# A block of seven products in a gated MLP: two weight quadrants loaded earlier, two down pieces moved ahead of the last product, the gate turned in one

## The chip, the cores and the metric

The kernel runs on one core of a Trainium2 chip. The metric is the device time of one execution in microseconds (us), taken as the median of several runs. One execution was also profiled by the hardware; its span runs from the first to the last instruction, and its own time is a little longer than its span. Engines are named as in the profile: PE does matmuls (PEld loads their weights), DVE and ACT work on tensors element by element, POOL does little here, SP issues nearly all DMAs.

## The reference

The reference is an encoder of two layers on 256 tokens of 1024 channels, in float32. Each layer has a token mixer and then a gated MLP; only the MLP matters here:

```python
def _conv_ffn(xn, w_up, conv_w, conv_b, w_down):
    a, gval = jnp.split(xn @ w_up, 2, axis=-1)
    a = lax.conv_general_dilated(a, conv_w[:, None, :], window_strides=(1,),
                                 padding=((CONV_WIDTH // 2, CONV_WIDTH // 2),),
                                 dimension_numbers=('NWC', 'WIO', 'NWC'),
                                 feature_group_count=D_FF) + conv_b
    return (jax.nn.gelu(a) * gval) @ w_down
```

`w_up` is 1024 x 5632 (2816 columns for `a`, 2816 for the gate), `w_down` 2816 x 1024. `setup_inputs` draws all weights at random.

## The kernel before

**Two parts for every number.** A float32 weight is read from memory as a `raw` tile (1 MB: two pieces of 128 x 1024), and each piece is split into a rounded part `wh` (a cast on ACT, line 252) and the rest `wl` (a subtraction on DVE, line 254). PE multiplies with both: wh by x's high part, wl by x's high part, wh by x's low part. So one piece costs ACT a cast, DVE a subtraction and PE 12 matmuls of 512 columns (6 where only one half of the tokens is multiplied). There are 3 raw buffers and 5 buffers each for `wh` and `wl`; a piece can be split only when PE has finished with the piece five places earlier. A raw load with a tag goes into another, named tile and takes none of the 3 buffers.

**Order.** The middle of each layer is written out by hand: `tc.manual_schedule()` keeps every engine's instructions in the order in which the Python code makes them. The order of the weight pieces is the order of the `W.use` calls, and the order of the loads that of the `W.add` calls (through `rows`); a load is issued as soon as it is within reach of the piece that is split next. SP issues DMAs in that order and stands still at one whose buffer is not free.

**The MLP's groups.** `MLP_GROUPS` lists them: `g` and `a` groups are 512 columns of the gate half and of the `a` half of `w_up` (four pieces, line 750), `w` is the block, `b` a mixed rest group, `d` are pieces of `w_down`. After a group its result is turned on DVE (line 804, "crossing"), written to DRAM in chunks (line 809) and read back with channels on partitions (line 816, into `zga` and `zg`). For each pair of 128-channel chunks f there are then five steps at places that `PAIR_PLACES` gives: on ACT `fetch_up` (lines 1487 and 1489) and the GELU (1497), on DVE `neighbours` (1493, 1494), `gate` (1501), then a cast on ACT (1509) and a rest on DVE (1510). A "place" is one piece of work of PE; the first is 8.

**The block.** Group 3 of both halves together is a 2 x 2 product of quadrants, computed with seven products instead of eight (`block` for the weights, `block_units` for the products, line 1579): "11", "T1", "22", "T2", "21", "T3", "T4". T1 to T4 take sums of weight quadrants, which DVE makes in the raw tiles (line 342) just before the piece is split. Quadrants "11" and "12" (first row block of `w_up`; 11 of the gate half, 12 of the `a` half) lie in the tagged tiles `ybig` and `at2`; T1 needs both. Four PSUM banks of the pool `mmp` serve groups and block; the block's are p (11, 21: first half of the gate), t and q. `add(0)`, `add(1)` on DVE (line 1604, tile `kept`) add a bank to a kept one and turn the result; T3 and T4 write on into the bank q that `add(0)` and `add(1)` read. `BLOCK` gives the order of the products and of eight `w_down` pieces "d" (lines 667 to 669, `res_ps`) in between, and the dictionary `after` what follows each product.

Of the kernel before, what the change touches and what calls it, by code (L numbers as in the profile page):

```python
# [26 lines left out]
DFF = 2816  # L27
# [262 lines left out]
def encoder(ctx, tc, x, w_in, w_pool, pool_scale, w_a, w_b, w_o, norm1, norm2, w_up, conv_w,  # L290
# [11 lines left out]
    W = Weights(tc, wpool, big, sm)  # L302
# [16 lines left out]

    def block(w, down, n):  # L320

        def quadrant(k, c0, tag=None):
            return rows(w, k * 512, 4, c0, 512, tag)

        gate, act = DFF + n * 512, n * 512
        made = {"11": quadrant(0, gate, "ybig"), "12": quadrant(0, act, "at2")}
        d = rows(down, 0) + rows(down, 2 * P)
        made["22"] = quadrant(1, act)
        d += rows(down, 4 * P)
        made["21"] = quadrant(1, gate)  # L330
        d += rows(down, 6 * P)
# [3 lines left out]
        def raw(name, j):  # L335
            return W.raw[made[name][0][0]][:, 2 * j : 2 * j + 2]
# [11 lines left out]
        k = 0  # L348
        for unit in BLOCK:
            if unit == "d":  # L350
                W.use([d[k]])
                k += 1
                continue
            name, j = unit
            if name in SUMS:
                sum_later(len(W.pieces), SUMS[name], j)
            if name in terms:
                W.use([(d[k][0], lambda t, name=name, j=j: raw(name, j), (2, 512))])
            else:
                W.use([made[name][j]])  # L360

    first_up = []
    for l in range(DEPTH):
# [659 lines left out]
    for l in range(DEPTH):  # L1023
# [527 lines left out]
        def block_units(n):  # L1551
# [50 lines left out]
            def add(t):  # L1602
# [75 lines left out]
```

## Time and profile before

| what | value |
|---|---|
| median of 3 runs | 862.76 us (861.73 to 863.35) |
| the profiled execution | 863.14 us, its span 861.3 us |
| granted TensorE clock, mean | 0.997 |
| DVE `wl` (L254) | 286 of 1217 ns, 343.8 us busy |
| ACT `wh` (L252) | 286 of 1048 ns, 296.0 us busy |
| chain that ended last | PE 80%, DVE 10%, DMA 5% |
| DMA | 214.03 MB, mean 248 GB/s |

Busy times overlap between engines, so they don't add up to the span. In a timeline row the first number is the start in us from the start of the span, the second the time from the first instruction's start to the last one's end, then engine, line, operation and tiles, and in brackets the idle time before it with what ended it. In a row of windows, after the stretch and its length, stand the busy time and count of PE, PEld, DVE, ACT and POOL, then PE's granted clock, the DMA engines' busy share and the GB/s moved. A row of the chain has start, length and what.

### The profile page before, as it was taken

How to read it: one execution, taken by the hardware profiler on the slowest of the kernel's cores; microseconds unless marked ns; L12 is line 12 of the kernel's file. 1: busy time of each engine (PE TensorE's matmuls, PEld its weight loads, DVE VectorE, ACT ScalarE, POOL GpSimd, SP SyncE). 2: the span in 40 equal slices, each digit the busy share in tenths (PEclk: the TensorE clock that was granted, in tenths of full speed). 3: DMA queues.
4: the chain of work that ended last, by engine and by line, in shares of the span. 5: the costliest groups of instructions: out<-in, count | busy, mean ns of one | idle time of the engine just before them, and what ended most of it. 6: DMA issues, size and time to landing. Idle time of an engine off the chain costs nothing.

```text
span 861.3 us, 10959 instructions
## 1 busy us (share of the span) xinstructions
PE 845.2 (98%) x3901; PEld 702.3 (82%) x3901; DVE 645.2 (75%) x838; ACT 522.6 (61%) x757; POOL 35.1 (4%) x96
## 2 busy tenths in 40 slices
PE   9999999999999989999999999999999999899997
PEld 7888888888888868788888888888888888687886
DVE  6958877766777679887765687868567876998774
ACT  7735556644565766677645454577454656767683
POOL 1710000000010000000010000000000100000000
PEclk9999999999999999999999999999999999999999
DMA  8699986886738866788736899768776499667861
GB/s 302 218 299 304 325 269 210 280 281 225 251 137 305 289 239 218 231 292 284 260 127 199 265 276 328 250 223 269 242 264 248 147 308 313 215 215 246 295 241 50
DMA packets 147967, 214.03 MB, mean 248 GB/s; under 512 B 7800, under 2 KB 69184, under 8 KB 147912
## 3 DMA queue, kind: packets, MB, share of 16 engines
q1 hardware_dynamic: 147480, 212.67, 74.6%
q8 instruction: 31, 0.51, 0.2%
q10 hardware_dynamic: 432, 0.66, 0.2%
q14 instruction: 24, 0.20, 0.1%
HBM read 186.02 MB, written 27.28 MB: 248 GB/s over the span
## 4 chain that ended last, share of the span: by engine, by line
PE 80%; DVE 10%; DMA 5%; ACT 2%; issue 2%; SPq 0%; POOL 0%; ACTq 0%; DVEq 0%; POOLq 0%
PE t_ps L750 50%; PE v_ps L750 6%; DVE wl L254 5%; PE res_ps L668 5%; PE res_ps L667 5%; PE res_ps L669 5%; DMA raw<-in_w_up_dram 3%; PE v_ps L1003 3%; DVE raw L342 2%; PE pool_ps L654 1%; PE v_ps L902 1%; DMA crossing<-crossing 1%; PE t_ps L1579 1%; PE o_ps L1286 1%; PE s_ps L1238 1%
## 5 line engine op out<-in xcount | busy, mean ns | idle before, releaser
L254 DVE TENSOR_TENSOR wl<-raw,wh 128x1024 fp32r<-128x1024 f32 x286 | 343.8, 1217 | 109.5 <-ACT wh L252 108.6
L750 PE MATMUL t_ps<-wh,x 128*128 128x512 f32 x1280 | 399.5, 390 | 0.0
L252 ACT CAST wh<-raw 128x1024 fp32r<-128x1024 f32 x286 | 296.0, 1048 | 169.5 <-PE t_ps L750 103.0
L750 PEld LDWEIGHTS t_ps<-wh,x 128*128 128x128 f32 x1280 | 240.3, 188 | 49.8
L750 PE MATMUL t_ps<-wl,x 128*128 128x512 f32 x640 | 249.1, 389 | 0.0
L750 PEld LDWEIGHTS t_ps<-wl,x 128*128 128x128 f32 x640 | 120.2, 188 | 25.1 <-DVE wl L254 0.2
L668 PE MATMUL res_ps<-wl,actq 128*128 128x512 f32 (+1 forms) x184 | 70.1, 381 | 1.7 <-DVE wl L254 1.7
L667 PE MATMUL res_ps<-wh,actq 128*128 128x512 f32 (+1 forms) x184 | 70.2, 382 | 1.3 <-ACT wh L252 1.3
L669 PE MATMUL res_ps<-wh,actk 128*128 128x512 f32 (+1 forms) x184 | 69.3, 380 | 0.0
L668 PEld LDWEIGHTS res_ps<-wl,actq 128*128 128x128 f32 x184 | 34.6, 188 | 8.9 <-DVE wl L254 2.3
L667 PEld LDWEIGHTS res_ps<-wh,actq 128*128 128x128 f32 x184 | 34.6, 188 | 8.8 <-ACT wh L252 2.2
L750 PE MATMUL t_ps<-wh,po 128*128 128x512 f32 x128 | 41.4, 395 | 0.0
L669 PEld LDWEIGHTS res_ps<-wh,actk 128*128 128x128 f32 x184 | 34.6, 188 | 6.5
L1489 ACT ACTIVATE a<-zga,prm 128x256 f32<-128x256 f32 x80 | 38.9, 512 | 0.0
L544 POOL TENSOR_SCALAR ss<-ss 128x1 f32<-128x1 f32 x8 | 2.1, 265 | 779.4 <-ACT junk L537 779.4
L804 DVE STREAM_TRANSPOSE crossing<-t_ps 128x512 f32<-128x512 f32 x36 | 23.9, 694 | 6.7 <-DMA crossing<-crossing 6.7
L342 DVE TENSOR_TENSOR raw<-raw,raw 128x1024 f32<-128x1024 f32 x16 | 19.5, 1217 | 12.7 <-DMA raw<-in_w_up_dram 12.7
L750 PEld LDWEIGHTS t_ps<-wh,po 128*128 128x128 f32 x128 | 24.0, 188 | 4.9
L1497 ACT ACTIVATE y<-y 128x512 f32<-128x512 f32 x22 | 13.9, 633 | 21.3 <-DVE y L1494 21.3
L667 PE MATMUL res_ps<-wh,m 128*128 128x512 f32 (+1 forms) x72 | 26.5, 367 | 0.0
L668 PE MATMUL res_ps<-wl,m 128*128 128x512 f32 (+1 forms) x72 | 26.3, 365 | 0.0
L669 PE MATMUL res_ps<-wh,m 128*128 128x512 f32 (+1 forms) x72 | 26.0, 366 | 0.0
(211 smaller groups left out, 1067.4 us busy)
## 6 DMA issues: line engine op xcount, KB each, us to landing
raw<-in_w_in_dram SPq DMA_DIRECT2D x58, 1024.0 KB
raw<-in_w_up_dram SPq DMA_DIRECT2D x40, 1024.0 KB
raw<-in_w_down_dram SPq DMA_DIRECT2D x22, 1024.0 KB
crossing<-crossing SPq DMA_DIRECT2D x22, 512.0 KB
crossing<-way SPq DMA_DIRECT2D x16, 512.0 KB
raw<-in_w_a_dram SPq DMA_DIRECT2D x8, 1024.0 KB
raw<-in_w_o_dram SPq DMA_DIRECT2D x8, 1024.0 KB
zga<-crossing SPq DMA_DIRECT2D x40, 128.0 KB
```

The source lines that it names most:

```text
L252: inst = nc.scalar.copy(out=h, in_=src)
L254: inst = self.rests[i] = nc.vector.tensor_sub(out=l, in0=src, in1=h.bitcast(F32))
L342: nc.vector.tensor_sub(out=raw(name, j), in0=raw(one, j), in1=raw(other, j))
L654: nc.tensor.matmul(out, w(k), x, start=(steps is first and k == 0), stop=(steps is last and k == nk - 1), skip_group_check=turns["rest"],)
L667: nc.tensor.matmul(ps, ah, wh, start=first, stop=False, skip_group_check=on)
L668: nc.tensor.matmul(ps, ah, wl, start=False, stop=False, skip_group_check=on)
L669: nc.tensor.matmul(ps, al, wh, start=False, stop=last, skip_group_check=on)
L750: nc.tensor.matmul(ps, x2[:, 2 * n + j, part, t, :], w[:, j, :], start=(n + m == 0), stop=(n == last and m == 5),)
L804: nc.vector.transpose(out=y.rearrange("p q c j -> p c q j"), in_=rows)
L1003: nc.tensor.matmul(ps[t], a[:, k, t, :], w[:, j, :], start=(k + m == 0), stop=(k == KD - 1 and m == 2),)
L1489: nc.scalar.mul(out=out, in_=a, mul=row(j, c))
L1497: nc.scalar.activation(t["y"], t["y"], AF.Gelu_apprx_tanh)
```

## The change

Four edits, the same in both layers.

1. The loads of quadrants 11 and 12 are added before the pieces of group `a` 2 instead of behind group `g` 2; `quadrant` and `first_quadrants` are taken out of `block` for that.
2. In `BLOCK` the last "d" moves from behind T4 to ahead of it: T3, d, d, T4 instead of T3, d, T4, d.
3. The first half of the gate (bank p) is no longer turned behind T3 but behind T4, together with the second half.
4. In `PAIR_PLACES` the pair f = 8 moves from places (39, 41), inside the block, to (46, 48), behind it; f = 10, 12 and 14 move by one slot each, f = 14 now having (55, 57).

```diff
 PAIR_PLACES = (
-    (11, 14), (14, 16), (19, 22), (21, 23), (39, 41), (46, 48), (49, 51), (52, 54), (60, 62), (63, 65), (58, 60),
+    (11, 14), (14, 16), (19, 22), (21, 23), (46, 48), (49, 51), (52, 54), (55, 57), (60, 62), (63, 65), (58, 60),
 )
 BLOCK = (
     ("11", 0), ("11", 1), "d", ("T1", 0), ("T1", 1), "d", "d", ("22", 0), ("22", 1), "d", ("T2", 0), ("T2", 1), "d",
-    ("21", 0), ("21", 1), "d", ("T3", 0), ("T3", 1), "d", ("T4", 0), ("T4", 1), "d",
+    ("21", 0), ("21", 1), "d", ("T3", 0), ("T3", 1), "d", "d", ("T4", 0), ("T4", 1),
 )
...
-    def block(w, down, n):
-
-        def quadrant(k, c0, tag=None):
-            return rows(w, k * 512, 4, c0, 512, tag)
-
-        gate, act = DFF + n * 512, n * 512
-        made = {"11": quadrant(0, gate, "ybig"), "12": quadrant(0, act, "at2")}
+    def quadrant(w, n, k, gate, tag=None):
+        return rows(w, k * 512, 4, gate * DFF + n * 512, 512, tag)
+
+    def first_quadrants(w, n):
+        return {"11": quadrant(w, n, 0, 1, "ybig"), "12": quadrant(w, n, 0, 0, "at2")}
+
+    def block(w, down, n, made):
+        made = dict(made)
...
         for kind, n in MLP_GROUPS:
+            if (kind, n) == ("a", 2):
+                corner = first_quadrants(w_up[l], 3)
             if kind == "w":
-                block(w_up[l], w_down[l], n)
+                block(w_up[l], w_down[l], n, corner)
...
-                "T3": (lambda: add(1), lambda: turn("g", 0, banks["p"])), "T4": (lambda: turn("g", 1, banks["q"]),),
+                "T3": (lambda: add(1),), "T4": (lambda: turn("g", 0, banks["p"]), lambda: turn("g", 1, banks["q"])),
```

On SP, at the start of the first layer's MLP, before (2444 to 2535 are raw tiles of `w_up` for the groups a 1, g 1 and the first of a 2; `crossing` is a group's result on its way out, `zga` its way back):

```order
L412 DMA gain<-in_norm_dram 128x1024
L171 DMA raw_2444<-in_w_up_dram 128x4x512
L809 DMA crossing<-crossing 128x2x512
L816 DMA zga<-crossing 32x8x128 x4
L171 DMA raw_2466<-in_w_up_dram 128x4x512
L171 DMA raw_2500<-in_w_up_dram 128x4x512
L809 DMA crossing<-crossing 128x2x512
L171 DMA raw_2535<-in_w_up_dram 128x4x512
```

and with the change, in the same place on SP, where 2535 and 2537 are now quadrants 11 and 12 and 2539 is the first tile of a 2:

```order
L415 DMA gain<-in_norm_dram 128x1024
L171 DMA raw_2535<-in_w_up_dram 128x4x512
L171 DMA raw_2444<-in_w_up_dram 128x4x512
L812 DMA crossing<-crossing 128x2x512
L171 DMA raw_2537<-in_w_up_dram 128x4x512
L819 DMA zga<-crossing 32x8x128 x4
L171 DMA raw_2466<-in_w_up_dram 128x4x512
L171 DMA raw_2500<-in_w_up_dram 128x4x512
L812 DMA crossing<-crossing 128x2x512
L171 DMA raw_2539<-in_w_up_dram 128x4x512
```

Quadrant 11 now stands ahead of the last raw tile of a 1, and quadrant 12 ahead of the reads that bring group a 0 back.

On SP, shortly ahead of the block, before (2662 is the last tile of g 2, 2719 and 2725 are quadrants 11 and 12, 2727 and 2764 hold the first four down pieces):

```order
L171 DMA raw_2662<-in_w_up_dram 128x4x512
L809 DMA crossing<-crossing 128x2x512
L171 DMA raw_2719<-in_w_up_dram 128x4x512
L816 DMA zg<-crossing 32x8x128 x4
L171 DMA raw_2725<-in_w_up_dram 128x4x512
L171 DMA raw_2727<-in_w_down_dram 128x2x1024
L171 DMA raw_2764<-in_w_down_dram 128x2x1024
L809 DMA crossing<-crossing 128x2x512
```

and with the change, in the same place on SP (2666 is the last tile of g 2, 2723 and 2764 hold the down pieces):

```order
L171 DMA raw_2666<-in_w_up_dram 128x4x512
L812 DMA crossing<-crossing 128x2x512
L171 DMA raw_2723<-in_w_down_dram 128x2x1024
L819 DMA zg<-crossing 32x8x128 x4
L171 DMA raw_2764<-in_w_down_dram 128x2x1024
L812 DMA crossing<-crossing 128x2x512
```

Both quadrant loads are gone from here, and a down tile has the place of the first.

On DVE, at the end of the first layer's block, before (3126 and 3151 are T4's two pieces, 3164 the last d's; `y`, `g` and `actk` are the pair f = 8; the last `kept` is `add(1)`; the transposes behind it turn its result and bank p):

```order
L254 TENSOR_TENSOR wl_3126<-raw_2725,wh_3125 128x1024
L1493 TENSOR_TENSOR y<-y,a_3141 128x2x255
L1494 TENSOR_TENSOR y<-y,a_3143 128x2x255
L254 TENSOR_TENSOR wl_3151<-raw_2725,wh_3150 128x1024
L1501 TENSOR_TENSOR g<-y,zg 128x512
L254 TENSOR_TENSOR wl_3164<-raw_3006,wh_3163 128x1024
L1510 TENSOR_TENSOR actk_2427<-g,actq_2425 128x512
L1604 TENSOR_TENSOR kept<-t_ps,kept 128x512
L804 STREAM_TRANSPOSE crossing<-kept 128x4x4x32
L804 STREAM_TRANSPOSE crossing<-t_ps 128x4x4x32
```

and with the change, in the same place on DVE (3126 is the last d's piece, 3142 and 3152 are T4's, 3162 to 3216 the four of the group b):

```order
L254 TENSOR_TENSOR wl_3126<-raw_3006,wh_3125 128x1024
L254 TENSOR_TENSOR wl_3142<-raw_2537,wh_3141 128x1024
L254 TENSOR_TENSOR wl_3152<-raw_2537,wh_3151 128x1024
L1607 TENSOR_TENSOR kept<-t_ps,kept 128x512
L807 STREAM_TRANSPOSE crossing<-kept 128x4x4x32
L254 TENSOR_TENSOR wl_3162<-raw_3087,wh_3161 128x1024
L254 TENSOR_TENSOR wl_3188<-raw_3087,wh_3187 128x1024
L254 TENSOR_TENSOR wl_3204<-raw_3090,wh_3203 128x1024
L254 TENSOR_TENSOR wl_3216<-raw_3090,wh_3215 128x1024
L807 STREAM_TRANSPOSE crossing<-t_ps 128x4x4x32 x2
```

The four instructions of f = 8 have left the stretch ahead of `add(1)`, and the gate's two transposes stand together behind the pieces of group b.

More of the change, by code (lines that the diff above doesn't have):

```diff
@@ L318, in of_both @@
         )
[L320 to L326 removed]
+    def quadrant(w, n, k, gate, tag=None):
[4 more added lines that the diff above has]
+        made = dict(made)
         d = rows(down, 0) + rows(down, 2 * P)
[L328 removed]
+        made["22"] = quadrant(w, n, 1, 0)
         d += rows(down, 4 * P)
[L330 removed]
+        made["21"] = quadrant(w, n, 1, 1)
         d += rows(down, 6 * P)
@@ L356, in block @@
                 sum_later(len(W.pieces), SUMS[name], j)
-            if name in terms:
-                W.use([(d[k][0], lambda t, name=name, j=j: raw(name, j), (2, 512))])
+            if name in ("22", "21"):
+                W.use([made[name][j]])
             else:
-                W.use([made[name][j]])
+                W.use([(d[min(k, 7)][0], lambda t, name=name, j=j: raw(name, j), (2, 512))])
     first_up = []
```

## The prediction

> **What bounds the kernel now.** I read the totals first, then the chain that ended last, then PE's own timeline.
>
> ```profile
> span 861.3 us, 10959 instructions
> PE 845.2 (98%) x3901; PEld 702.3 (82%) x3901; DVE 645.2 (75%) x838; ACT 522.6 (61%) x757; POOL 35.1 (4%) x96
> ...
> 257.87 40.42 PE t_ps L750 x179
> 361.00 32.64 PE t_ps L750 x144
> ```
>
> The first two lines are totals, the other two pieces of the chain. PE is the bound, so only a change that takes idle or slow time from PE can shorten the kernel. The last row gives PE's pitch when nothing is in its way: 32.64 us / 144 = 0.2267 us from one matmul to the next. With that pitch each stage's PE time is known, and what a stage takes beyond it is lost. In the block PE does 14 half products of 6 matmuls and 8 down pieces of 12, so 180 matmuls, or 40.8 us. The first and last of them, in both layers, and the rows at which PE waited:
>
> ```profile
> 312.11 0.39 PE L1579 MATMUL t_ps<-wh,x 128*128 128x512 f32 x1
> 316.40 0.50 PE L667 MATMUL res_ps<-wh,actq 128*128 128x512 f32 x1 [0.87 <-ACT wh L252]
> 317.73 0.50 PE L668 MATMUL res_ps<-wl,actq 128*128 128x512 f32 x1 [0.82 <-DVE wl L254]
> 321.38 0.47 PE L1579 MATMUL t_ps<-wh,sx 128*128 128x512 f32 x1 [0.86 <-DVE crossing L804]
> 351.25 0.39 PE L669 MATMUL res_ps<-wh,actk 128*128 128x512 f32 x1
> 353.72 0.77 PE L1579 MATMUL t_ps<-wh,x 128*128 128x512 f32 x1 [2.08 <-DVE kept L1604]
> 360.83 0.39 PE L750 MATMUL t_ps<-wh,x 128*128 128x512 f32 x1
> ...
> 737.83 0.39 PE L1579 MATMUL t_ps<-wh,x 128*128 128x512 f32 x1
> 746.16 0.47 PE L1579 MATMUL t_ps<-wh,sx 128*128 128x512 f32 x1 [0.87 <-DVE crossing L804]
> 778.49 0.47 PE L1579 MATMUL t_ps<-wh,x 128*128 128x512 f32 x1 [2.08 <-DVE kept L1604]
> 784.05 0.39 PE L750 MATMUL t_ps<-wh,x 128*128 128x512 f32 x1
> ```
>
> The block takes 360.83 - 312.11 = 48.72 us in the first layer and 784.05 - 737.83 = 46.22 us in the second, so **7.9 and 5.4 us are lost, 13.3 us together**. Three places hold them. *Start*: up to T1's first matmul (321.38 and 746.16) there are 24 matmuls, 5.44 us; PE took 9.27 and 8.33, a loss of 3.8 and 2.9. *End*: from there to T4's first matmul (353.72 and 778.49) there are 132 matmuls, 29.92 us; it took 32.34 and 32.33, a loss of 2.4 in each. *After T4's start*, 24 matmuls: 7.11 and 5.56 for 5.44, a loss of 1.7 in the first layer and 0.1 in the second. The windows name that last one, by the clock column (the third number from the end; the first row is the whole block of the first layer):
>
> ```profile
> 312.10:360.80 48.70, 44.01 (x181) 34.52 (x180) 44.11 (x48) 34.01 (x45) 0.00 (x0) 0.96 0.62 202
> 353.55:356.95 3.40, 3.23 (x8) 2.59 (x9) 0.73 (x2) 0.52 (x2) 0.00 (x0) 0.52 0.52 163
> 778.40:781.80 3.40, 3.31 (x15) 2.75 (x16) 0.69 (x1) 1.42 (x3) 0.00 (x0) 1.00 0.54 167
> ```
>
> After the same wait the granted clock was about half for 3.4 us in the first layer, and full in the second.
>
> The Trainium skill, "TensorE: Matmul & The Clock Gate", Part 1 (The HAM clock gate), says that the clock is halved after an idle window of about 3.4 us that runs freely, so that the same kernel can meet it or not. Here a wait of 2.46 us between matmul starts (351.25 to 353.72) was enough once and not the other time. By that rule a wait that stays may cost 1.7 us in either layer, where the rows have it in one.
>
> Why PE waited is told by DVE, where both waits end:
>
> ```profile
> 305.10 1.23 DVE L342 TENSOR_TENSOR raw<-raw,raw 128x1024 f32<-128x1024 f32 x1 [6.80 <-DMA raw<-in_w_up_dram]
> 320.53 1.30 DVE L804 STREAM_TRANSPOSE crossing<-t_ps 128x512 f32<-128x512 f32 x2
> 348.02 0.68 DVE L1493 TENSOR_TENSOR y<-y,a 128x510 f32<-128x510 f32 x1
> 352.29 0.68 DVE L1510 TENSOR_TENSOR actk<-g,actq 128x512 fp32r<-128x512 f32 x1
> 352.89 0.68 DVE L1604 TENSOR_TENSOR kept<-t_ps,kept 128x512 f32<-128x512 f32 x1
> 729.88 1.22 DVE L342 TENSOR_TENSOR raw<-raw,raw 128x1024 f32<-128x1024 f32 x1 [5.86 <-DMA raw<-in_w_up_dram]
> 745.30 1.30 DVE L804 STREAM_TRANSPOSE crossing<-t_ps 128x512 f32<-128x512 f32 x2
> ```
>
> T1's first sum stood idle 6.80 us (5.86 in the second layer) for quadrant 12, and held up everything that follows it on DVE, down to the transposes of group g 2 that free T1's bank. At the other end `add(1)` ran at 352.89, behind f = 8, and T4 may not write into its bank before.
>
> **Part 1, the early loads: the start.** Without that DMA wait DVE's chain moves up 6.80 and 5.86 us. The first of g 2's transposes (half of 1.30, so 0.65) then ends at 320.53 + 0.65 - 6.80 = 314.4, and in the second layer at 745.30 + 0.65 - 5.86 = 740.1. PE at full pitch wants T1's bank at 312.11 + 5.44 = 317.55, and at 737.83 + 5.44 = 743.27. Both are met with 3 us to spare; g 2's own matmuls end where the block begins, so they don't hold the transposes. The cast and rest at which PE waited at 316.40 and 317.73 hang on the same chain. So the start's 3.8 + 2.9 = **6.7 us go**. What is late next is nothing at T1; DVE would have to slip another 3 us.
>
> What the two loads cost where they now stand is told by the chain's row for group a 0, SP's timeline, three windows (the last two numbers are the DMA share and GB/s), ACT's timeline and the page's groups (the number behind the comma is the mean in ns):
>
> ```profile
> 252.40 5.47 PE v_ps L750 x24
> ...
> 257.25 0.37 SPq L171 DMA_DIRECT2D raw<-in_w_up_dram  x1
> 259.61 0.37 SPq L809 DMA_DIRECT2D crossing<-crossing  x1
> 263.74 1.81 SPq L816 DMA_DIRECT2D zga<-crossing  x4
> 265.66 1.23 SPq L171 DMA_DIRECT2D raw<-in_w_up_dram  x2
> ...
> 258.90:263.00 4.10, 4.10 (x20) 3.40 (x19) 4.10 (x7) 3.12 (x4) 0.00 (x0) 1.00 0.96 369
> 263.00:264.90 1.90, 1.90 (x10) 1.59 (x9) 1.90 (x3) 1.05 (x1) 0.00 (x0) 1.00 0.05 16
> 267.00:276.00 9.00, 9.00 (x41) 7.47 (x40) 5.93 (x7) 3.23 (x4) 0.00 (x0) 1.00 1.01 381
> ...
> 270.86 2.00 ACT L252 CAST wh<-raw 128x1024 fp32r<-128x1024 f32 x2 [3.69 <-DMA raw<-in_w_up_dram]
> ...
> L254 DVE TENSOR_TENSOR wl<-raw,wh 128x1024 fp32r<-128x1024 f32 x286 | 343.8, 1217 | 109.5 <-ACT wh L252 108.6
> L252 ACT CAST wh<-raw 128x1024 fp32r<-128x1024 f32 x286 | 296.0, 1048 | 169.5 <-PE t_ps L750 103.0
> ```
>
> Quadrant 11 needs `ybig`, which holds the second of group a 0's four pieces. PE leaves it half way through the 24 matmuls that start at 252.40, at about 255.1, before SP issues the next raw load at 257.25: SP's stop there costs nothing. `at2` holds the third piece and is free about 256.5, before SP has passed the crossing at 259.61. A load is 1.05 MB, at 369 to 381 GB/s 2.8 us. The first finds the queue empty from 255.1; the second falls into the hole at 263.0 to 264.9 (share 0.05), where SP waits for a crossing to land, and pushes the reads behind it by 2.8 - 1.9 = 0.9 us. At worst both stand fully in the way, 5.6 us. The first raw tile of g 1 is then ready for ACT at 270.86 + 5.6 = 276.5 instead of 270.86. PE starts g 1 at 257.87 plus 96 matmuls, 279.6; cast and rest (1048 and 1217 ns) need 2.3 us, so the slack is 279.6 - 2.3 - 270.86 = **6.4 us**. I take 0 for PE; the lower bound is 0, since PE has no idle time there to give back, and the upper one, both loads fully in the way, is 0 too, as 5.6 is under 6.4. The second layer does the same work in the same order, and I take the same. Ahead of the block the queue loses the same two loads.
>
> **Part 2, the second d ahead of T4, and f = 8 out of the block: the end.** Between T3 and T4 PE now has two down pieces, 5.44 us, instead of one, 2.72. The wait there was 2.4 us, so the second d covers it by itself, with 0.3 to spare. f = 8 takes four DVE instructions of 0.68 us, starting at 348.02 and ending with the row at 352.29, from in front of `add(1)`: 2.4 to 2.7 us more. And DVE arrives up to 6.8 us earlier. What bounds `add(1)` then is PE: T4's second piece waits for T3's first buffer, which PE leaves after 138 matmuls, at 312.11 + 31.28 = 343.4; cast, rest and `kept` (1.05 + 1.22 + 0.68) put its end at 346.4. PE wants T4 after 168 matmuls, at 350.2. Margin 3.8 us, so the end's 2.4 + 2.4 go, and with the wait the half clock and the 0.1 behind it: **6.6 us**.
>
> **Part 3, the gate turned in one.** The same two transposes, later. They hold two banks until just behind T4; by the order of instructions group a 4 is the first that waits for them, a whole group b (48 matmuls, 10.9 us) later, and two transposes take 1.30. Cost 0; without that cover 1.3 us a layer.
>
> **Part 4, f = 8 behind the block.** Its work goes into groups b, a 4 and g 4, three windows of 10.9 us (DVE's busy time is the third, ACT's the fourth after the length), with the longest of its ACT instructions from the page's groups:
>
> ```profile
> 360.80:371.70 10.90, 10.90 (x49) 9.01 (x48) 10.16 (x12) 9.33 (x16) 0.00 (x0) 1.00 0.96 308
> 371.70:382.60 10.90, 10.90 (x50) 9.02 (x49) 7.68 (x10) 8.39 (x15) 0.00 (x0) 1.00 0.74 267
> 382.60:393.50 10.90, 10.90 (x50) 9.03 (x49) 8.41 (x10) 5.68 (x7) 0.00 (x0) 1.00 0.81 277
> ...
> L1497 ACT ACTIVATE y<-y 128x512 f32<-128x512 f32 x22 | 13.9, 633 | 21.3 <-DVE y L1494 21.3
> ```
>
> DVE has 26.3 of 32.7 us there and gets 2.7; ACT has 23.4 and gets eight instructions of at most 0.633, so under 5.1. Both still fit (29.0 and 28.5), and PE, which does not wait there, comes in with up to five pieces split ahead. Cost 0; with the cover gone, at most ACT's 5.1 a layer.
>
> **The sum.** 6.7 + 6.6 = 13.3 us, all that PE loses in the two blocks, against the profiled execution's 863.14 us (its span 861.3 and 1.8 around it): **849.8 us**. The median of the runs before, 862.76, is 0.4 us lower; a run without the half clock would be 1.7 lower, so the ratio to the median is a little smaller.
>
> **Rivals.**
> *Half of it.* Only the end goes, because something other than quadrant 12 also holds T1's sum; or only the start, because DVE, 44.11 us busy of 48.70 in the block, can't keep its lead. That gives 863.14 - 6.6 = 856.5 or 863.14 - 6.7 = 856.4. Against the first: the wait at 305.10 is put down to a DMA of `w_up`. Against the second: the second d alone covers the end. 0.08 and 0.07.
> *The edit does not do what it says*: SP or the queue brings the quadrants no sooner in effect and DVE's lag moves to the next sum. 863, for which only DVE's load speaks: 0.05.
> *The early loads starve g 1, and the kernel is slower.* From 257 to 276 the queue is full (share 1.01), so a delay may not be made up. It decides at 6.4 us: beyond, PE waits in both layers, and the whole gain is gone once the delay is 6.4 + 6.65 = 13.1 us, with the two loads at about 160 GB/s instead of 370. At a delay of 14 us the time is 849.8 + 2 x 7.6 = 865.0. The hole at 263 and the 6.4 us speak against it: 0.05.
>
> The Trainium skill, "DMA: Bandwidth & Descriptors", section "Queues, rings and completion order", says that descriptors of one ring are consumed in order, so a load put in front delays all that SP issued behind it. That is this rival's mechanism; no row before separates it from SP's own waits. By the page's limit for one core's memory, about 358 GB/s (Specifications), the two loads would take an estimated 5.9 us instead of 5.6; the row at 381 GB/s is above that limit. Neither reaches the slack.
>
> **Chances and range.** Forecast, both ends go: 0.75, with a range of its own of 848.8 to 852 (0.2% or 1.7 us is about what a measurement of this kernel can tell from no change; small waits of some tenths may stay, and the median before is 0.4 lower). The halves reach to 857.0, which together is 0.90; a cut at 852 would leave out 0.25. So 848.8 to 857.0. Faster by over 0.2%: 0.75 + 0.15 = 0.90; within: 0.05; slower: 0.05.
>
> **What would show it.** Right: T1's sum on DVE has no DMA wait ahead of it; T1's first matmul comes 5.4 to 5.6 us after the block's first; `kept` ends over 3 us ahead of T4; the block's windows show 40.8 to 41.2 us and a full clock. Wrong: PE rows in g 1 or a 2 that wait for a cast (early loads too dear), an idle row on DVE at the sum that another load ended, a wait at T4 for `kept`, or one in a 4 or g 4 for f = 8.

## The result and the profile after

| | median | runs |
|---|---|---|
| before | 863.06 us (861.73 to 867.08) | 4 |
| changed | 849.89 us (849.66 to 851.33) | 4 |

The ratio is 0.9843, with a 95% interval of 0.9809 to 0.9878: 1.6% faster. Forecast was 849.8 us. The profiled execution of the changed kernel took 851.33 us (span 849.5 and 1.8 around it), which makes it the longest of its four. So its trace shows a little that the other runs may not have. Of all runs reported below one was slow, the second of six of "loads and f = 8" (1320.13 us at a granted clock of 0.60), and its ratio leaves it out.

The totals of the changed kernel and the engines of its chain of waits:

```profile
span 849.5 us, 10951 instructions
PE 840.6 (99%) x3901; PEld 700.9 (83%) x3901; DVE 645.6 (76%) x838; ACT 523.8 (62%) x757; POOL 34.0 (4%) x96
...
PE 89%; DMA 4%; DVE 4%; ACT 1%; issue 1%; SPq 0%; POOL 0%; ACTq 0%; DVEq 0%; POOLq 0%
```

PE has 89% of the chain where it had 80%, and DVE 4% where it had 10%. PE's timeline has the same places as before: the block's first matmul, the waits, T1's first, T4's first and the first behind the block (lines of the changed kernel are higher by 3):

```profile
312.03 0.39 PE L1582 MATMUL t_ps<-wh,x 128*128 128x512 f32 x1
315.38 0.50 PE L671 MATMUL res_ps<-wl,actq 128*128 128x512 f32 x1 [0.25 <-DVE wl L254]
319.04 0.47 PE L1582 MATMUL t_ps<-wh,sx 128*128 128x512 f32 x1 [0.87 <-DVE crossing L807]
351.83 0.39 PE L1582 MATMUL t_ps<-wh,x 128*128 128x512 f32 x1
354.55 0.39 PE L753 MATMUL t_ps<-wh,x 128*128 128x512 f32 x1
...
731.51 0.39 PE L1582 MATMUL t_ps<-wh,x 128*128 128x512 f32 x1
736.96 0.39 PE L1582 MATMUL t_ps<-wh,sx 128*128 128x512 f32 x1
769.60 0.39 PE L1582 MATMUL t_ps<-wh,x 128*128 128x512 f32 x1
772.32 0.39 PE L753 MATMUL t_ps<-wh,x 128*128 128x512 f32 x1
```

In the second layer no row waits: the block takes 772.32 - 731.51 = 40.81 us, which is 180 matmuls at full pitch. In the first it takes 42.52. T1 comes 7.01 us after the first matmul instead of 5.44, so 1.57 us of start loss are left, and some 0.14 behind it. T4 waits in neither layer. The windows of the two blocks say the same (clock third from the end):

```profile
312.03:354.55 42.52, 41.40 (x182) 33.55 (x180) 40.33 (x42) 28.34 (x33) 0.00 (x0) 1.00 0.64 207
731.51:772.32 40.81, 40.81 (x182) 33.79 (x181) 37.44 (x38) 25.28 (x27) 0.00 (x0) 1.00 0.60 202
```

No half clock is left in either block. Together they took 94.94 us before and take 83.33 now: 11.61 of the 11.81 us between the two profiled executions (863.14 and 851.33).

DVE's timeline at T1's first sum, at g 2's transposes and at `add(1)`, in both layers:

```profile
302.78 1.22 DVE L343 TENSOR_TENSOR raw<-raw,raw 128x1024 f32<-128x1024 f32 x1
318.19 1.31 DVE L807 STREAM_TRANSPOSE crossing<-t_ps 128x512 f32<-128x512 f32 x2
347.95 0.68 DVE L1607 TENSOR_TENSOR kept<-t_ps,kept 128x512 f32<-128x512 f32 x1
...
718.60 1.22 DVE L343 TENSOR_TENSOR raw<-raw,raw 128x1024 f32<-128x1024 f32 x1
734.01 1.30 DVE L807 STREAM_TRANSPOSE crossing<-t_ps 128x512 f32<-128x512 f32 x2
765.22 0.68 DVE L1607 TENSOR_TENSOR kept<-t_ps,kept 128x512 f32<-128x512 f32 x1
```

T1's sum no longer waits for a DMA. But in the first layer it starts at 302.78, only 2.3 us sooner than the 305.10 of before, where the prediction had 6.8. Why is seen on SP, first before the change and then with it:

```profile
263.74 1.81 SPq L816 DMA_DIRECT2D zga<-crossing  x4
269.96 0.37 SPq L809 DMA_DIRECT2D crossing<-crossing  x1
274.69 1.81 SPq L816 DMA_DIRECT2D zg<-crossing  x4
276.59 0.40 SPq L171 DMA_DIRECT2D raw<-in_w_up_dram  x1
```

```profile
266.08 1.81 SPq L819 DMA_DIRECT2D zga<-crossing  x4
269.88 0.37 SPq L812 DMA_DIRECT2D crossing<-crossing  x1
279.83 1.81 SPq L819 DMA_DIRECT2D zg<-crossing  x4
281.74 0.40 SPq L171 DMA_DIRECT2D raw<-in_w_up_dram  x1
```

SP issues the second `crossing` at the same time as before, but the reads `zg`, which wait until it has landed, go out 5.1 us later, and the tile of a 2 behind them too. ACT's timeline in the changed kernel shows the tiles landing late:

```profile
275.87 2.00 ACT L252 CAST wh<-raw 128x1024 fp32r<-128x1024 f32 x2 [8.78 <-DMA raw<-in_w_up_dram]
290.61 1.05 ACT L252 CAST wh<-raw 128x1024 fp32r<-128x1024 f32 x1 [3.56 <-DMA raw<-in_w_up_dram]
```

The first cast of g 1 is at 275.87 instead of 270.86. The cast of the third piece of a 2, at 290.61, waited for a DMA as well, and T1's sum follows it 12.2 us later. Before the change that cast was 5.5 us sooner and waited for PE:

```profile
285.11 1.05 ACT L252 CAST wh<-raw 128x1024 fp32r<-128x1024 f32 x1 [0.65 <-PE t_ps L750]
```

PE did not wait in g 1 or a 2. So two of the signs that the prediction named for being right, T1 within 5.6 us and a block of at most 41.2 us, are missing in the first layer of this profile and there in the second.

### The profile page after: what moved, and what is told of

It is laid out like the page before. It is cut to its first block, busy times and chain, and to the rows that moved or that the text cites. A ratio compares the mean times of both kernels' runs of the same rounds, so it can differ in the third digit from the quotient of the medians.

```text
span 849.5 us, 10951 instructions
## 1 busy us (share of the span) xinstructions
PE 840.6 (99%) x3901; PEld 700.9 (83%) x3901; DVE 645.6 (76%) x838; ACT 523.8 (62%) x757; POOL 34.0 (4%) x96
## 4 chain that ended last, share of the span: by engine, by line
PE 89%; DMA 4%; DVE 4%; ACT 1%; issue 1%; SPq 0%; POOL 0%; ACTq 0%; DVEq 0%; POOLq 0%
PE t_ps L753 53%; PE res_ps L670 6%; PE res_ps L671 6%; PE res_ps L672 6%; PE v_ps L753 6%; PE t_ps L1582 4%; PE v_ps L1006 3%; DMA raw<-in_w_up_dram 2%; DVE wl L254 1%; PE pool_ps L657 1%; PE v_ps L905 1%; DMA crossing<-crossing 1%; PE o_ps L1289 1%; PE s_ps L1241 1%; PE s_ps L1236 1%; PE o_ps L1285 1%
## 5 line engine op out<-in xcount | busy, mean ns | idle before, releaser
L540 ACT ACTIVATE junk<-h 128x512 f32<-128x512 f32 (+1 forms) x19 | 10.5, 554 | 25.2 <-DVE h L562 25.0
L1496 DVE TENSOR_TENSOR y<-y,a 128x510 f32<-128x510 f32 x22 | 14.9, 679 | 14.1 <-ACT y L1490 14.1
L753 PE MATMUL v_ps<-wh,x 128*128 128x512 f32 x80 | 25.7, 392 | 0.0
```

Of the source, the lines that this page charges most:

```text
L540: nc.scalar.activation(junk[:, 0 : cc.stop - cc.start], h[:, t, cc], AF.Square, scale=D**-0.5, accum_out=ss[:, n : n + 1],)
L753: nc.tensor.matmul(ps, x2[:, 2 * n + j, part, t, :], w[:, j, :], start=(n + m == 0), stop=(n == last and m == 5),)
L1496: nc.vector.tensor_add(out=y[:, :, 1:], in0=y[:, :, 1:], in1=t["a0"][:, :, : S - 1])
```

## The experiments

All times are medians; each ratio is against runs of the kernel before on the same chip, whose medians were 864.7 to 865.2 us there (863.06 for the first profile of the changed kernel). "Start" is the time from the block's first matmul to T1's first, less 5.44 us. "Lead" is how long before the block's first matmul DVE starts T1's first sum. Both stand for the first / second layer of the profiled execution. "End only", "second d only" and "f = 8 only" are the changed kernel with both quadrant loads put back to the block, and with the other edits that are not named taken back; the edits below are shown against the kernel before.

| kernel | median us | ratio (95%) | lead | start loss |
|---|---|---|---|---|
| before, first profile | 863.06 | | 7.01 / 7.95 | 3.84 / 2.88 |
| changed, first profile | 849.89 | 0.9843 (0.9809 to 0.9878) | 9.25 / 12.91 | 1.57 / 0 |
| changed, second | 849.87 | 0.9833 (0.9809 to 0.9857) | 11.44 / 11.84 | 0 / 0 |
| changed, third | 850.34 | 0.9842 (0.9819 to 0.9864) | 11.77 / 10.09 | 0 / 0.76 |
| loads only | 855.97 | 0.9907 (0.9885 to 0.9929) | 11.31 / 8.79 | 0 / 2.03 |
| end only | 858.15 | 0.9930 (0.9910 to 0.9951) | 7.06 / 7.13 | 3.78 / 4.27 |
| second d only | 863.59 | 0.9990 (0.9971 to 1.0008) | 7.91 / 7.56 | 2.94 / 3.29 |
| f = 8 only | 857.82 | 0.9926 (0.9902 to 0.9950) | 6.27 / 7.58 | 5.13 / 3.28 |
| changed, f = 8 in the block | 850.93 | 0.9847 (0.9823 to 0.9871) | 11.68 / 11.20 | 0 / 0 |
| loads and f = 8 | 850.17 | 0.9830 (0.9807 to 0.9854) | 11.05 / 13.74 | 0 / 0 |
| changed, gate turned apart | 850.75 | 0.9844 (0.9822 to 0.9866) | 11.23 / 10.49 | 0 / 0.34 |
| both quadrants at g 2 | 852.70 | 0.9859 (0.9834 to 0.9884) | 9.59 / 9.65 | 1.25 / 1.19 |
| quadrant 11 at a 2, 12 at g 2 | 853.71 | 0.9887 (0.9858 to 0.9916) | 11.33 / 9.66 | 0 / 1.18 |
| early loads doubled | 862.97 | 0.9978 (0.9959 to 0.9996) | 8.57 / 8.05 | 2.26 / 2.78 |

### The early loads alone

```diff
         for kind, n in MLP_GROUPS:
+            if (kind, n) == ("a", 2):
+                corner = first_quadrants(w_up[l], 3)
...
-                block(w_up[l], w_down[l], n)
+                block(w_up[l], w_down[l], n, corner)
```

> The early quadrant loads alone; the order of T3, d, T4, d, the gate's turns and f = 8 stay as before. Theory (start and end are two separate losses): in both layers the wait at T1 goes or shrinks to the 1.3 us that the changed kernel kept in its first layer, while the wait at T4 for `kept` stays at 1.0 to 2.4 us; 863.1 - 6.7 = 856.4, up to 858. Rival 1 (DVE's lead alone would have been enough, the end's edits do nothing): the waits at T4 go too, 850 to 852. Rival 2 (DVE's rate through the block sets its end, so what PE gains at T1 it waits for at T4): the waits at T4 grow to 5 us or more and the time stays at 862 to 863.

855.97 us, 0.9907: the theory's size, and the waits at T4 stayed. The timelines of DVE and PE at T4 in the first layer:

```profile
348.50 0.69 DVE L1607 TENSOR_TENSOR kept<-t_ps,kept 128x512 f32<-128x512 f32 x1
...
349.33 0.47 PE L1582 MATMUL t_ps<-wh,x 128*128 128x512 f32 x1 [1.80 <-DVE kept L1607]
```

PE's waits in this kernel, summed over the span (total, times, longest), have one such wait in each layer:

```profile
PE t_ps L1582 <- DVE kept L1607: 3.9, 2, 2.1
```

And the window of the 3.4 us behind the second layer's wait has a clock of 0.51:

```profile
773.10:776.50 3.40, 3.40 (x9) 2.64 (x9) 0.26 (x1) 1.04 (x1) 0.00 (x0) 0.51 0.75 230
```

So start and end are two losses, and the lead on DVE does not pay for both. From the sum (300.70) to `add(1)` DVE took 47.8 us, the same as in the kernel before (305.10 to 352.89). With the wait came the half clock again, this time in the second layer.

### The three edits of the end, without the early loads

```diff
-    (11, 14), (14, 16), (19, 22), (21, 23), (39, 41), (46, 48), (49, 51), (52, 54), (60, 62), (63, 65), (58, 60),
+    (11, 14), (14, 16), (19, 22), (21, 23), (46, 48), (49, 51), (52, 54), (55, 57), (60, 62), (63, 65), (58, 60),
-    ("21", 0), ("21", 1), "d", ("T3", 0), ("T3", 1), "d", ("T4", 0), ("T4", 1), "d",
+    ("21", 0), ("21", 1), "d", ("T3", 0), ("T3", 1), "d", "d", ("T4", 0), ("T4", 1),
...
-                "T3": (lambda: add(1), lambda: turn("g", 0, banks["p"])), "T4": (lambda: turn("g", 1, banks["q"]),),
+                "T3": (lambda: add(1),), "T4": (lambda: turn("g", 0, banks["p"]), lambda: turn("g", 1, banks["q"])),
```

> The second d ahead of T4, the gate turned in one and f = 8 behind the block, with the quadrant loads where they were before. Theory: the waits at T4 (2.4 us in each layer) go, and the half clock behind the first of them; the waits ahead of T1 stay at 2.9 to 3.8 us a layer: 863.1 - 6.6 = 856.5. Rival (the start's lag on DVE is what made the end late, and the end's edits are not enough without the early loads): a wait at T4 of over 1 us stays, 858 to 861.

858.15 us, 0.9930: on the scale of the 863.06 of before that is 857.0, the theory's 856.5 within the interval. The waits at T4 were gone in both layers; the start lost 3.78 and 4.27 us.

### The second d alone

```diff
-    ("21", 0), ("21", 1), "d", ("T3", 0), ("T3", 1), "d", ("T4", 0), ("T4", 1), "d",
+    ("21", 0), ("21", 1), "d", ("T3", 0), ("T3", 1), "d", "d", ("T4", 0), ("T4", 1),
```

> The second d ahead of T4 alone, with f = 8 still in front of `add(1)`, the gate's first half turned behind T3 and the loads as before. Theory: the second d puts 2.72 us in front of T4 where the wait was 2.4, so the end's 6.6 us go with it alone: 856.5 as in the kernel with all three end edits, `kept` ending 0 to 0.5 us ahead of T4. Rival 1 (the d's own pieces are cast and rested on DVE ahead of `add(1)`, 1.2 us each, so that `add(1)` slips by as much as the second d covers): a wait of 1 to 2.4 us stays at T4, 860 to 863.

863.59 us, 0.9990: nothing, and neither theory had the reason. T4 indeed did not wait, but PE now waited at the first matmuls behind the block. The timelines of DVE around `add(1)` in the first layer and of PE at its first wait behind the block:

```profile
304.10 1.22 DVE L343 TENSOR_TENSOR raw<-raw,raw 128x1024 f32<-128x1024 f32 x1 [5.90 <-DMA raw<-in_w_up_dram]
...
351.90 0.69 DVE L1607 TENSOR_TENSOR kept<-t_ps,kept 128x512 f32<-128x512 f32 x1
352.62 0.71 DVE L807 STREAM_TRANSPOSE crossing<-kept 128x512 f32<-128x512 f32 x1
356.76 0.72 DVE L807 STREAM_TRANSPOSE crossing<-t_ps 128x512 f32<-128x512 f32 x1 [3.43 <-DMA crossing<-crossing]
357.40 1.18 DVE L254 TENSOR_TENSOR wl<-raw,wh 128x1024 fp32r<-128x1024 f32 x1
...
358.64 0.50 PE L753 MATMUL t_ps<-wl,x 128*128 128x512 f32 x1 [2.35 <-DVE wl L254]
```

PE's waits summed have it in both layers:

```profile
PE t_ps L753 <- DVE wl L254: 4.5, 2, 2.4
```

Behind `add(1)` stands bank p's transpose. It waits 3.43 us for a DMA of `crossing`: the tile that it writes has the same single buffer (tag `v0`) as the one that is just taking the result of `add(1)` out. The rests of group b are queued behind it. With "d" behind T4, PE had that piece to work on meanwhile; with both d's in front, it runs into group b 2.72 us sooner. This is what the third edit of the change takes care of: with the gate turned behind T4, DVE makes the rests of b first.

### f = 8 alone

```diff
-    (11, 14), (14, 16), (19, 22), (21, 23), (39, 41), (46, 48), (49, 51), (52, 54), (60, 62), (63, 65), (58, 60),
+    (11, 14), (14, 16), (19, 22), (21, 23), (46, 48), (49, 51), (52, 54), (55, 57), (60, 62), (63, 65), (58, 60),
```

> The pair f = 8 behind the block alone; T3, d, T4, d and the loads as before. Theory: four DVE instructions of 0.68 us leave the stretch in front of `add(1)`, which then starts 2.4 to 2.7 us sooner; the wait at T4 (2.4 us) shrinks to 0 to 0.5 us and with it the half clock: 856.5 to 858. Rival (what holds `add(1)` is the rest piece behind T3's buffer, which PE leaves late, and the instructions of f = 8 only fill DVE's idle time): the wait at T4 stays at 1.5 to 2.4 us, 861 to 863.

857.82 us, 0.9926, with no wait at T4 in either layer: the theory, and as much as all three end edits together. DVE's timeline at the two ends of its stretch in the first layer:

```profile
306.87 1.23 DVE L343 TENSOR_TENSOR raw<-raw,raw 128x1024 f32<-128x1024 f32 x1 [7.54 <-DMA raw<-in_w_up_dram]
...
352.06 0.69 DVE L1607 TENSOR_TENSOR kept<-t_ps,kept 128x512 f32<-128x512 f32 x1
```

45.19 us instead of 47.8: f = 8 is worth 2.6 us in front of `add(1)`, as priced.

### The changed kernel with f = 8 in the block

```diff
-    (11, 14), (14, 16), (19, 22), (21, 23), (46, 48), (49, 51), (52, 54), (55, 57), (60, 62), (63, 65), (58, 60),
+    (11, 14), (14, 16), (19, 22), (21, 23), (39, 41), (46, 48), (49, 51), (52, 54), (60, 62), (63, 65), (58, 60),
```

> The changed kernel with f = 8 back at places (39, 41), inside the block; the early loads, the second d and the gate as changed. Theory as the prediction had it (the second d covers the end by itself): as the changed kernel, 849.7 to 851.5. Rival, from the kernel with the second d alone (there the wait at T4 was gone, but the first matmuls of group b waited 2.6 and 2.7 us for their rest pieces, 2.7 and 4.1 us lost with the half clock): DVE is as far behind at the block's end as before, with only another piece to show it, and 2.5 to 4 us a layer stand at the first or second matmul of group b: 855 to 857.

850.93 us, 0.9847, within the intervals of the changed kernel; no wait at T4, none in group b. The rival fell. DVE's timeline at `add(1)`:

```profile
348.19 0.68 DVE L1607 TENSOR_TENSOR kept<-t_ps,kept 128x512 f32<-128x512 f32 x1
348.91 0.71 DVE L807 STREAM_TRANSPOSE crossing<-kept 128x512 f32<-128x512 f32 x1
349.55 4.59 DVE L254 TENSOR_TENSOR wl<-raw,wh 128x1024 fp32r<-128x1024 f32 x4
354.05 1.31 DVE L807 STREAM_TRANSPOSE crossing<-t_ps 128x512 f32<-128x512 f32 x2
```

Here b's four rests come right behind `add(1)` and end at 354.1; the gate's transposes come last. This kernel differs from the one with the second d alone by the early loads and by the gate. The early loads don't take the transpose's wait away, for the kernel with the loads alone, whose gate is turned in two, has it in its first layer too:

```profile
353.77 0.72 DVE L807 STREAM_TRANSPOSE crossing<-t_ps 128x512 f32<-128x512 f32 x1 [3.85 <-DMA crossing<-crossing]
```

So it is the gate's place that lets b's rests go first. The kernel with both d's in front, the early loads, f = 8 in the block and the gate in two was not timed. By the 5.50 us from `add(1)` to b's first rest in the kernel with the second d alone (351.90 to 357.40), that rest would end there at an estimated 348.19 + 5.50 + 1.18 = 354.9, where PE wants it at 353.12, one matmul behind the block's end at 352.89.

### The early loads and f = 8, without the second d and with the gate in two parts

```diff
-    ("21", 0), ("21", 1), "d", ("T3", 0), ("T3", 1), "d", "d", ("T4", 0), ("T4", 1),
+    ("21", 0), ("21", 1), "d", ("T3", 0), ("T3", 1), "d", ("T4", 0), ("T4", 1), "d",
...
-                "T3": (lambda: add(1),), "T4": (lambda: turn("g", 0, banks["p"]), lambda: turn("g", 1, banks["q"])),
+                "T3": (lambda: add(1), lambda: turn("g", 0, banks["p"])), "T4": (lambda: turn("g", 1, banks["q"]),),
```

> The early loads and f = 8 behind the block, with T3, d, T4, d and the gate's first half turned behind T3 as before: the changed kernel without its second and third edit. Theory, from the runs with one edit each: these two do all of it, no wait at T4, 849.7 to 851.5, the same as the changed kernel. Rival (the second d is needed where the start is early, since PE then wants T4 sooner): a wait of 1 to 2.4 us at T4 for `kept` in each layer, 852 to 856.

850.17 us, 0.9830: the changed kernel without two of its edits, and as fast. Both blocks took 40.8 us. The end has two remedies in the change, f = 8 moved or the second d with the gate in one, and either is enough beside the early loads.

### The gate apart

```diff
-                "T3": (lambda: add(1),), "T4": (lambda: turn("g", 0, banks["p"]), lambda: turn("g", 1, banks["q"])),
+                "T3": (lambda: add(1), lambda: turn("g", 0, banks["p"])), "T4": (lambda: turn("g", 1, banks["q"]),),
```

> The changed kernel with the gate's first half turned behind T3 as before. Theory (part 3 costs and brings nothing: there is cover on both sides): as the changed kernel within 0.2%, no wait in the block or in group b. Rival (0.65 us more of DVE in front of the last pieces of the block, which then come late for T4 or the first matmul of group b): 0.3 to 1.3 us a layer, 850.5 to 852.5.

850.75 us, 0.9844, against 0.9842 of the changed kernel in the same set: no difference, as the theory has it. Bank p's transpose waits here too, 3.54 us, but with the early loads and f = 8 out of the block DVE is so early that b's first rest starts at 351.88, and group b's first matmul comes at 353.12 without a wait.

### The changed kernel again, twice

> The changed kernel itself, as the measure for the other three of this set on the same chip. Expected from its first runs: 0.9843 of the kernel before, 849.5 to 851.5 beside a before of 863; over several profiles the wait ahead of T1 that its first layer showed (1.6 us) may stand in either layer or in none, since the loads-only kernel had it in the second layer (2.0) and not in the first.

> The changed kernel once more, as the measure for the other three of this set: 0.983 to 0.985 of the kernel before. From the traces so far the start loss follows the lead of T1's first sum on DVE ahead of the block's first matmul: 10.83 us minus the lead, and nothing where the lead is longer (lead 7.0, loss 3.84; 9.25, 1.57; 11.05 and more, 0). Expected here: a lead between 9 and 13 us in each layer, and a loss in either that this difference gives within 0.1 us.

849.87 and 850.34 us. The second profile (849.51 us) is the one the prediction describes: the two blocks' windows have the full clock and no loss.

```profile
312.01:352.81 40.80, 40.80 (x181) 33.80 (x180) 38.75 (x40) 26.40 (x29) 0.00 (x0) 1.00 0.62 205
729.78:770.58 40.80, 40.80 (x181) 33.78 (x180) 38.44 (x39) 26.00 (x28) 0.00 (x0) 1.00 0.63 206
```

The third lost 0.76 us at the second layer's start, with a lead of 10.09: the difference to 10.83 is 0.74, as expected.

### The quadrants one group later

```diff
-            if (kind, n) == ("a", 2):
+            if (kind, n) == ("g", 2):
                 corner = first_quadrants(w_up[l], 3)
```

> The changed kernel with quadrants 11 and 12 taken ahead of the last pieces of group g 2 instead of those of a 2, one group later than changed and still sooner than before. Theory (the early loads push the tiles of g 1 and a 2 behind them by up to 5 us, and this is what leaves up to 1.6 to 2.0 us of start loss in one layer): ACT's first cast of g 1 comes back to about 271 us, as before the change; if the quadrants still land ahead of T1's sum the start loss is 0 in both layers and the time 848.5 to 850, up to 0.2% under the changed kernel. Rival (the later loads now stand in front of the tiles of g 2 and the block's first down pieces, or land after T1's sum wants them): T1's sum waits for a DMA again, 1 to 4 us lost ahead of T1 in each layer, 852 to 857.

852.70 us, 0.9859. ACT's two casts that waited, and between them SP's row in which three loads stand together:

```profile
270.93 2.00 ACT L252 CAST wh<-raw 128x1024 fp32r<-128x1024 f32 x2 [3.79 <-DMA raw<-in_w_up_dram]
...
288.51 1.50 SPq L171 DMA_DIRECT2D raw<-in_w_up_dram  x3
...
296.72 1.05 ACT L252 CAST wh<-raw 128x1024 fp32r<-128x1024 f32 x1 [5.40 <-DMA raw<-in_w_up_dram]
```

Half of the theory held: g 1's first cast is back at 270.93. But quadrant 11 now took the issue place of g 2's first tile, which had to stand behind the next read-back, with quadrant 12, at 288.51. ACT waited 5.40 us for it, and T1's sum had a lead of 9.6 us in both layers. No DMA row stands ahead of the sum itself; the rival had the price for a layer (1.2 us) and not the place.

### The two loads apart

```diff
             if (kind, n) == ("a", 2):
-                corner = first_quadrants(w_up[l], 3)
+                corner = {"11": quadrant(w_up[l], 3, 0, 1, "ybig")}
+            if (kind, n) == ("g", 2):
+                corner["12"] = quadrant(w_up[l], 3, 0, 0, "at2")
```

> The changed kernel with the two loads apart: quadrant 11 ahead of the pieces of a 2 as changed, quadrant 12 ahead of those of g 2. Theory (each load delays the tiles behind it by up to 2.8 us, and what decides is how long DVE has before the block to win that back): ACT's first cast of g 1 at 271 to 273.5, a lead of T1's sum between that of the kernel with both loads late (9.6 in both layers, loss 1.2) and that of the changed kernel (9.3 to 12.9), so 0 to 1.2 us lost a layer: 849.7 to 852.3. Rival (the delay adds up only when both loads stand at one place): lead over 11 in both layers, no loss, 849.5 to 850, no run above 850.5.

853.71 us, 0.9887, no better than either placement of both, and above what either theory gave. The profiled execution (852.81, the shortest of its runs) lost 1.18 us at the second layer's start and began its first block at 313.94, 1.9 us later than the first profile of the changed kernel (312.03), lost in the first 12 us of the program, in which these loads have no part. What the longer runs, up to 856.95, lost was not seen.

### The early loads doubled

```diff
                 else:
                     self.nc.sync.dma_start(out=t, in_=src)
+                if self.n_loaded in self.again:
+                    self.nc.sync.dma_start(out=self.spare[self.n_loaded % 2], in_=src)
```

> The changed kernel with each of the two early quadrant loads followed by a second transfer of the same 1.05 MB, to a place in DRAM that nothing reads: the cost of the early loads doubled. Theory (a load put in front delays the stream behind it by its own length, less the holes it fills; PE has 6.4 us of slack at g 1): ACT's first cast of g 1 comes 8 to 11 us later than before the change instead of 2.5 to 5, PE waits 2 to 5 us a layer in g 1 for the first time, and T1's sum keeps a lead of 5 to 9 us, so 2 to 5 us a layer are lost at T1 as well unless the wait in g 1 gives the stream the time back: 853 to 862. Rival (most of the delay is SP's wait for the crossing and not the transfer itself, so the second transfer goes into holes): first cast of g 1 under 6.4 us later than before, no wait of PE in g 1, 849.7 to 852.

862.97 us, 0.9978: on the scale of 863.06 that is 861.2, inside the theory's 853 to 862, but by another way than it said. The scheduler did not put the second transfers behind the first ones; SP's timeline has one of them where quadrant 12 had been, quadrant 12 at the place of a 2's first tile (270.73), and that tile only at 282.49, where the changed kernel has it at 270.33. Then ACT's and PE's rows for it:

```profile
260.34 0.63 SPq L173 DMA_DIRECT2D spare<-in_w_up_dram  x1
...
270.73 0.80 SPq L171 DMA_DIRECT2D raw<-in_w_up_dram  x1
...
282.49 1.12 SPq L171 DMA_DIRECT2D raw<-in_w_up_dram  x2
...
291.31 1.04 ACT L254 CAST wh<-raw 128x1024 fp32r<-128x1024 f32 x1 [7.96 <-DMA raw<-in_w_up_dram]
...
292.41 0.50 PE L758 MATMUL t_ps<-wh,x 128*128 128x512 f32 x1 [1.59 <-ACT wh L254]
```

So it does not measure a doubled transfer. It does show the rival "starved" alive: PE waited at the first matmuls of a 2 in both layers, where the theory had g 1, the lead fell to 8.57 and 8.05, and nearly the whole gain was gone.

## Why the prediction was right, point by point

**The sum.** 13.3 us were to go from 863.14. The second profile of the changed kernel stands at 849.51 with both blocks at 40.80 us: 94.94 - 81.60 = 13.3 us less in the blocks than before. The bound (PE), the pitch and the block's 40.8 us held to a hundredth. What was left out is small: 0 to 1.6 us of start loss in some layers. In medians the gain was 13.2 us beside the first profile, and 14.8 and 14.4 us in the two later sets, whose runs of the kernel before were some 1.6 us longer; that the forecast lies within 0.1 us of the first median is partly luck.

**Part 1, the start: right mechanism, one term mis-sized.** All fourteen rows of the table follow one rule: start loss = 10.84 us - lead, and nothing where the lead is longer. Only two values stand off it by more than 0.03, both by 0.56 (the second layer of "end only", the first of "f = 8 only"), and in both a half clock fell into the start. The rule is DVE's own length: before, from the sum at 305.10 to the end of g 2's first transpose at 320.53 + 0.65 are 16.08 us, after (302.78, 318.19) 16.06; PE needs the bank 5.44 us after the block's start, and hears of it some 0.2 later. The prediction had this, and took the new lead as 7.0 + 6.8 = 13.8, 3 us more than needed. The leads of the changed kernel were 9.25 to 12.91. The step that failed is the delay of "2.8 - 1.9 = 0.9 us" on the tiles behind the two loads. Already the first read-back, `zga`, went out 2.3 us later (266.08 for 263.74), and g 1's first cast came 5.0 us late in the first profile (275.87 against 270.86), 2.6 in the second (273.50) and 5.1 in the third (275.98), inside the bounds of 0 to 5.6 but not near the value taken. I had counted only the queue behind the loads and missed the second turn: `crossing` waits in that queue too, and SP stops at `zg` until it has landed, so the next tile, the second of a 2, is not even issued (281.74 for 276.59). This tile, not the first one of g 1, sets T1's sum: in all six layers of the three profiles the sum follows the cast of a 2's third piece by 12.2 to 12.7 us, a stretch in which DVE works almost without pause. In the first layers that cast came at 290.61, 288.42 and 288.31 instead of 285.11, and the sum 4.5, 2.3 and 2.6 us behind the 298.30 that 305.10 - 6.80 gave. The sum of the prediction held because its margin was 3 us: it covered the delay in four of the six layers, and the other two lost 1.57 and 0.76 us. PE's own slack of 6.4 us at g 1 held: no wait of PE there in any of the profiles with the early loads as the change has them.

The Trainium skill, "DMA: Bandwidth & Descriptors", section "Queues, rings and completion order", says that on each DMA engine "descriptors are consumed in ring order". The trace is in line with it: `crossing`, issued at 269.88 instead of 269.96, let its reads go 5.1 us later when the two loads stood ahead. No row shows the order of the descriptors itself.

**Part 2, the end: the f = 8 half right, the d half wrong as it stood.** "The second d covers it by itself" is true of T4 and false of the time: alone it moved the wait behind the block (0.9990). f = 8 alone took the end away (0.9926). DVE's stretch shows why the end was late at all. From T1's sum to `add(1)` it takes 47.8 us with f = 8 and 45.2 without, with 1.2 us idle in it, as long as it is the later one; only with the longest leads does it catch up and wait for PE (46.6 us in the second layer of the changed kernel's first profile). While DVE holds T1 as well, T1's first matmul comes 10.84 + 5.44 = 16.28 after the sum, and `kept` ends 47.79 + 0.68 - 16.28 = 32.19 after T1's first matmul with f = 8, 29.6 without. PE wants T4 29.92 after it with one d, 32.64 with two. That gives a wait of 2.27 before (measured 2.24: 353.72 - 351.25 less one pitch), and margins of 0.3 for f = 8 alone, 0.45 for the second d alone, 3.0 for both. The prediction's bound, PE at 346.4, 34.3 us after the block's first matmul, holds only where DVE catches up: `kept` ended 34.4 to 34.5 us after it in four of the six layers of the changed kernel's profiles, and 35.8 and 36.6 in the two that had lost time at the start. So in the block of before DVE, not PE, set the pace; the prediction named it a rival (DVE "can't keep its lead") at 0.07, and for the kernel with the loads alone that is what happened.

**Part 3, the gate: 0 in the changed kernel, as priced, for a reason that was not seen.** Beside f = 8 it changes nothing (0.9844 against 0.9842). Bank p's transpose, where it stands behind `add(1)`, hangs on a DMA for 3.3 to 4.0 us in both layers of all six kernels that have it there, the kernel before among them, and b's rests with it. What differs is whether anyone notices: with the second d alone b's first rest started 1.5 us behind b's first matmul (357.40 against 355.90), with the early loads and f = 8 moved 1.2 us ahead of it. The prediction had looked only for who waits for the two banks, not at what the transposes themselves wait for.

**Part 4, f = 8 behind the block: 0, as priced.** From the end of group b, 48 matmuls behind the first block, to the start of the second block PE took 366.1 us before and 366.1 us with f = 8 moved, and a 4 and g 4 lie in that stretch. In the kernel with loads and f = 8 the first matmuls of group b lost 0.5 us, in the changed one nothing.

**The rivals.** "Half of it" did not come, and the two kernels with half of the change show its size: 0.9907 for the start, 0.9930 and 0.9926 for the end, with products of 0.9838 and 0.9834. "The edit does nothing" fell with T1's sum free of a DMA wait. "Starved, slower" did not come, but the doubled loads show that it was near by in kind: one more transfer at the wrong place gives the gain back.

No version timed here beats the changed kernel by more than the intervals. What the blocks can still give is the 0 to 1.6 us of start loss that differ from run to run.

## What to carry to other kernels

When a late engine is relieved of one wait, work out its own unbroken stretch from there to each place where the bound engine needs it: here 16.1 us to T1 and 45.2 or 47.8 to T4 gave the waits at both in every profile, but for two half clocks, and showed which edits are substitutes for each other. A load put early costs its bytes and also the issue place of whatever stood there: if the issuing engine stops at a read-back, the displaced tile comes a whole read-back later. When work is taken out between two waits, look at what the next instruction on the late engine waits for, not only at who waits for it.

## What the runs showed of the hardware

*Half clock after short waits.* A stretch of 3.4 us at a granted clock of about 0.5 followed three of the six single waits of 2.2 to 2.7 us (from one matmul's start to the next) at T4 or behind the block (before, first layer; loads only, second; second d only, second), and not the other three. Twice it came at a start, after two or three waits of 1.0 to 1.3 us each (end only, second layer; f = 8 only, first), and once in group a 2 behind waits of 2.0 and 1.3 us (doubled loads, first layer); in the other layers with such waits it did not. The Trainium skill, "TensorE: Matmul & The Clock Gate", Part 1, puts the halving behind an idle window of about 3.4 us; no wait here was that long.

*The same transfers, two lengths.* The second `crossing` of the first layer's MLP was issued at 269.88 and 269.87 in two profiles of the changed kernel, and its reads went out at 279.83 and 277.96. What makes the difference of 1.9 us was not found. It does not decide alone whether a run keeps its lead. In the third profile the reads went out late too (issued at 270.51, reads at 280.31), but the tile behind them was cast 6.1 us after its issue (282.22 to 288.31), where the first profile took 8.9 (281.74 to 290.61) and the second 8.6 (279.86 to 288.42), and the lead was 11.77.
